# The eighth product saved in the down-projection instead of the up-projection, tokens on partitions there, and a last norm along columns

## Chip, cores and metric

One core of a Trainium2 chip runs the whole program: 512 tokens through two layers, each a mixer (attention, then a recurrent block) and an MLP, and a last norm. The metric is the device time of one execution in microseconds. The engines are called TensorE (PE, matmuls; PEld its weight loads), VectorE (DVE), ScalarE (ACT), GpSimd (POOL) and SyncE (SP, which issues most DMAs).

## The reference

`SEQ` is 512, `D_MODEL` 1024, `D_FF` 4096. The mixers are not changed and are left out here.

```python
def rmsnorm(x, g):
    xf = x.astype(jnp.float32)
    y = xf * lax.rsqrt(jnp.mean(xf * xf, axis=-1, keepdims=True) + RMS_EPS)
    return (y * g.astype(jnp.float32)).astype(x.dtype)
...
def sq_relu_mlp(h, w1, w2):
    z = jax.nn.relu(jnp.einsum('bsd,df->bsf', h, w1))
    return jnp.einsum('bsf,fd->bsd', z * z, w2)
...
    for layer in range(DEPTH):
...
        h = h + mix
        h = h + sq_relu_mlp(rmsnorm(h, norm_mlp[layer]), mlp_w1[layer], mlp_w2[layer])
    return rmsnorm(h, norm_final)
```

## The kernel before

Everything is float32, and every matmul is made of three: a float is split into a high part, which TensorE takes at full rate, and a low part, the rest, and `mm3` (L203) adds high x high, low x high and high x low. So each weight block is cast by ScalarE to its high part (`wh`, L134), and VectorE subtracts to get the low part (`wl`, L137). A block is 512 KB, 128 partitions x 1024 numbers. `plan` is the list of blocks in the order of use; `fetch` (L100) issues the DMA of one on SyncE's queue, then its cast and subtraction, and `want` keeps `ahead` blocks (6 in an MLP, else 4) fetched ahead of the matmuls. Blocks called `wr` are used as they come; blocks called `b` are raw ones from which sums are formed first (L130, L131).

The residual stream lies in `h` as eight tiles of 128 columns (features) on partitions by 512 tokens. `hnH` and `hnL` are its parts scaled by the norm's gain; the norm's row 1/sqrt(mean square) is multiplied in later, since it belongs to the token. A norm that is `flat` sums squares over partitions by two matmuls with a matrix of ones and then takes a root and a reciprocal (L264) on tiles of 128 x 512, so that each partition holds the row. The other form gets one number per token on partitions (L269) and turns it into a row by four small matmuls (L282).

An MLP (`mlp`, L604) handles the 4096 hidden features in eight groups of 512. The first group's up-projection is plain. Each of the other seven treats its 1024 x 512 weights and the 1024 x 512 tokens as two by two blocks and forms **seven products of half-size blocks in place of eight**, by sums and differences of blocks. The products (tiles `p`) are 128 x 256, each from sums of token halves (`tH`, `tL`, made once per layer from `h` by `sums_of`) and sums of weight blocks (`b`). VectorE puts the seven products together (tiles `cA`, `cB`, L677 to L694), multiplies by the row (L654), ScalarE squares (L645), and `z` holds the split result. The down-projection (`down`, L698) is plain: for each group and each of 8 column tiles `d`, 12 matmuls of 512 tokens, whose result VectorE adds to `h` (L704). `up(g)` is a generator: between its products the column tiles of group g-1 are placed, two after the second product, one after the next four, two after the last.

At the end of layer 0, `down` of the last group feeds the next norm tile by tile (`n1.feed`). The recurrent block then makes eight tiles `xb`, a convolution of them on VectorE (`xp`, L819, `xc`, L825), two gates by small matmuls (`ga`, `gx`), a scan, eight tiles `yb`, the product `gd` (L869), and the output blocks `ro`, whose results are added to `h` (L921). In the last layer the last group's down-projection is done in token halves, so that the first half's last norm (`nf0`) runs beside the second half (`nf1`); outputs are stored with features on partitions and the host transposes them.

The order of instructions on each engine is set by a scheduler after the program is written, with TensorE's order near the written one. PSUM tiles come from two rings of four banks, `mmp` and `atp`. TensorE waits where a bank it would write has not been read.

Of the kernel before, what the change touches and what calls it, by code (L numbers as in the profile page):

```python
# [31 lines left out]
C_MIX0, C_MLP0, C_MIX1, C_MLP1, C_FIN = 0, 8, 16, 24, 32  # L32
C_BIN, C_CW, C_CB, C_BGA, C_BGX, C_AP, C_BO = 40, 56, 88, 96, 104, 112, 120
# [7 lines left out]
def trunk(ctx: ExitStack, tc: tile.TileContext, xT, cols, win, wqkv, wo, rwin, rga, rgx, rwo, w1, w2, out):  # L41
# [17 lines left out]
    cst = per.tile([P, P], F32, name="cst")  # L59
    hT = []  # L60


    def residual(name):
        both = [per.tile([P, 4, T], F32, name=f"{name}{i}", tag=f"hx{i}") for i in range(2)]
        hT[:] = [both[k // 4][:, k % 4] for k in range(KT)]

# [5 lines left out]
    onesR = per.tile([P, P], F32R, name="onesR")  # L72
    epsb = per.tile([P, 1], F32, name="epsb")
    spare = per.tile([P, 1], F32, name="spare")
    rt = per.tile([P, 4], F32, name="rt")
    sp4 = per.tile([P, KT], F32, name="sp4")
# [8 lines left out]
    V.tensor_copy(onesR, ones)  # L85
# [11 lines left out]
    state = {"next": 0, "ready": [], "ahead": 4, "stop": None, "more": None, "units": 0}  # L97
    raws, start_ = {}, []

    def fetch():  # L100
# [4 lines left out]
        if state["more"] is not None:  # L105
            pool = state["more"] if state["units"] % 8 >= 5 else wsp
            state["units"] += 1
# [3 lines left out]
        if kind == "plain":  # L111
            n = nk * sum(src.shape[1] for src in srcs)
            raw = wraw.tile([P, 1024], F32, name=f"wr{i}", tag="wr")
            rv = raw[:, :n].rearrange("p (k c) -> p k c", k=nk)
            c0 = 0
            for n_, src in enumerate(srcs):
                w = src.shape[1]
                queue = nc.scalar if i == 0 and n_ else nc.sync
                queue.dma_start(rv[:, :, c0 : c0 + w], src.rearrange("(k p) c -> p k c", p=P))
                c0 += w  # L120
        else:
            if kind == "11":
                for name, src in zip(("11", "21", "22", "12"), srcs):
                    raws[name] = state["raw"].tile([P, 1024], F32, name=f"b{name}_{i}", tag=f"b{name}")
                    nc.sync.dma_start(raws[name].rearrange("p (k c) -> p k c", k=4), src.rearrange("(k p) c -> p k c", p=P))

            for name, at_, with_ in (("s1", "21", "22"), ("s2", "22", "11"), ("s4", "12", "22")):
                if kind == name:
                    if kind == "s1":
                        V.tensor_add(raws["11"], raws["11"], raws["21"])  # L130
                    V.tensor_add(raws[at_], raws[at_], raws[with_])  # L131
            raw = raws[{"s1": "21", "s2": "22", "s3": "11", "s4": "12"}.get(kind, kind)]
# [40 lines left out]
    def add_mlp(layer):  # L173
        starts.append(len(plan))
        for g in range(9):
            if g == 0:
                add(w1[layer], 0, 0, KT)
                add(w1[layer], 0, U, KT)
                continue
            if g < 8:  # L180
                rows, cs = (slice(0, T), slice(T, D)), (slice(g * T, g * T + U), slice(g * T + U, (g + 1) * T))
                srcs = [w1[layer][rows[k], cs[c]] for k, c in ((0, 0), (0, 1), (1, 1), (1, 0))]
                up_ = [(kind, 4, srcs) for kind in ("11", "s1", "12", "22", "s2", "s4", "s3")]
            else:
                up_ = []
            dn = [("plain", 4, [w2[layer][(g - 1) * T : g * T, u * U : (u + 1) * U]]) for u in range(4)]
            if up_:
                plan.extend(up_[0:2] + dn[0:1] + up_[2:3] + dn[1:2] + up_[3:5] + dn[2:3] + up_[5:7] + dn[3:4])
            else:
                plan.extend(dn)  # L190

    add_mlp(0)
    for u in range(8):
        add(rwin, 0, u * U, KT)
# [8 lines left out]
    def mm3(acc, WH, WL, XH, XL, start, stop):  # L203
        PE.matmul(acc, WH, XH, start=start, stop=False)  # L204
        PE.matmul(acc, WH, XL, start=False, stop=False)  # L205
        PE.matmul(acc, WL, XH, start=False, stop=stop)  # L206

    def project(accs, cols_, WH, WL, xs, mid=None):

        for k, (XH, XL) in enumerate(xs):  # L210
            if mid and k == 1:
                mid()
            for acc, c in zip(accs, cols_):
                mm3(acc, WH(k, c), WL(k, c), XH, XL, k == 0, k == len(xs) - 1)
# [5 lines left out]
    class Norm:  # L220
        def __init__(self, name, gain, c0=0, n=T, late=False, flat=False):
            self.name, self.gain, self.acc, self.last, self.c, self.n = name, gain, None, None, slice(c0, c0 + n), n
            self.late, self.flat = late, flat
# [6 lines left out]
        def square(self, k, apart=False):  # L230
            if self.acc is None:
                self.acc = wk.tile([P, T], F32, name=f"{self.name}acc", tag="nacc")[:, : self.n]
                S.activation(self.acc, hT[k][:, self.c], AF.Square)
            else:
                sq = wk.tile([P, T], F32, name=f"{self.name}sq{k}", tag="nsq", bufs=2)[:, : self.n]
                if apart:
                    self.mark = V.tensor_mul(sq, hT[k][:, self.c], hT[k][:, self.c])
                    self.last = sq
                    return
                S.activation(sq, hT[k][:, self.c], AF.Square)  # L240
                V.tensor_add(self.acc, self.acc, sq)

        def feed(self, k):
            if k == 0:
# [5 lines left out]


        def sums(self, room=lambda name: wk.tile([P, T], F32R, name=name, tag="nsq", bufs=2)):
            nt = self.n // P
            ss = atp(f"{self.name}ss")
            if self.flat:
                ss = ss[:, : self.n]
                aH, aL = (room(f"{self.name}a{i}")[:, : self.n] for i in range(2))
                S.copy(aH, self.acc)
                V.tensor_sub(aL, self.acc, f(aH))
                PE.matmul(ss, onesR, aH, start=True, stop=False)  # L260
                PE.matmul(ss, onesR, aL, start=False, stop=True)
                self.r = wk.tile([P, T], F32, name=f"{self.name}r", tag="nr")[:, : self.n]
                S.activation(self.r, ss, AF.Sqrt, bias=epsb, scale=1.0 / D)
                V.reciprocal(self.r, self.r)  # L264
                return
            parts = [self.acc] if self.last is None else [self.acc, self.last]
            for n, part in enumerate(parts):
                for t in range(nt):
                    PE.matmul(  # L269
                        ss[:, 2 * t : 2 * t + 2], part[:, t * P : (t + 1) * P], ones[:, 0:2],  # L270
                        start=n == 0 and t == 0, stop=n == len(parts) - 1, skip_group_check=True,
                    )
            S.activation(rt[:, :nt], ss[:, 0 : 2 * nt : 2], AF.Sqrt, bias=epsb, scale=1.0 / D)
            self.mark = V.reciprocal(rt[:, :nt], rt[:, :nt])

        def rstd(self):
            if self.flat:
                return self.r
            nt = self.n // P
            row = atp(f"{self.name}row")  # L280
            for t in range(nt):
                PE.matmul(row[:, t * P : (t + 1) * P], rt[:, t : t + 1].to_broadcast([P, P]), ident, start=True, stop=True)  # L282
            if self.last is not None:
                return row[:, : self.n]
            r = wk.tile([P, T], F32, name=f"{self.name}r", tag="nr")[:, : self.n]
            S.copy(r, row[:, : self.n])
# [4 lines left out]
    nm1 = Norm("nm1", C_MLP0, late=True, flat=True)  # L291
    with ExitStack() as actx:
# [72 lines left out]
        def wo_tile(m, acc, last):  # L365
            V.tensor_add(hT[m], acc, hT[m])
            if last:
                nm1.feed(m)
# [235 lines left out]
    def mlp(ly, norm, nxt, halves):  # L604
        with ExitStack() as mctx:
            pool = lambda name, bufs: mctx.enter_context(tc.tile_pool(name=f"{name}{ly}", bufs=bufs))
            sr, wx, tp, cp, zp = pool("sr", 1), pool("wx", 3), pool("t", 1), pool("c", 1), pool("z", 2)
            state.update(raw=sr, more=wx, units=0, ahead=6, stop=starts[ly + 1] + 4 if ly + 1 < len(starts) else None)
            z, r, tH, tL = {}, [], [], []

            def sums_of(k):
                g, g2 = (cst[:, norm.gain + j : norm.gain + j + 1] for j in (k, k + 4))
                a = wk.tile([P, T], F32, name=f"ha{ly}{k}", tag="nsq", bufs=2)
                S.activation(a, hT[k], AF.Copy, scale=g)
                H = tp.tile([P, 4, U], F32R, name=f"tH{ly}{k}", tag=f"tH{k}")
                L = tp.tile([P, 4, U], F32R, name=f"tL{ly}{k}", tag=f"tL{k}")
                raw = zp.tile([P, 2, T], F32, name=f"ht{ly}{k}", tag=("zH0", "zH1", "zL0", "zL1")[k])
                raw = raw.rearrange("p i (j c) -> p (i j) c", j=2)

# [357 lines left out]
```

## Time and profile before

| | us |
|---|---|
| median of 3 runs | 1079.86 (1078.96 to 1079.87) |
| the profiled execution | 1079.9 |
| its span | 1078.1 |
| MLP of layer 0, first up matmul to first matmul of the recurrent block | 245.8 to 584.3 |
| recurrent block | 584.3 to 727.8 |
| MLP of layer 1, to its last matmul's start | 727.8 to 1068.0 |

The mean clock granted to TensorE is 0.997. A row of groups reads: line, engine, operation, output and inputs by the program's names, shape, count, then busy time, mean nanoseconds of one, and the engine's idle time ahead of them with what ended it. A row of the timeline has the start and the duration first, both in microseconds. Matmul durations overlap, so the step from one start to the next is what a matmul costs when TensorE does not wait.

### The profile page before, as it was taken

To read this page: it belongs to the slowest core of one execution; us is meant where nothing else is said; L and a number is where in the kernel's file an instruction comes from. 1 tells how busy PE (TensorE), PEld (TensorE's weight loads), DVE (VectorE), ACT (ScalarE), POOL (GpSimd) and SP (SyncE) were. 2 spreads that over 40 slices of the span, in tenths; PEclk is the share of its full clock that TensorE was granted. 3 is DMA by queue.
4 is the path that set the end of the run, shared out by engine and by line. 5 is a ranking of instruction groups with operands and counts; after the bars stand their busy time and mean duration, and the time that the engine had idled before them with its cause. 6 is when DMAs were issued, how large, how long until landed. Compare 5 with 4: busy or idle time off the path is not lost.

```text
span 1078.1 us, 15331 instructions
## 1 busy us (share of the span) xinstructions
PE 1067.4 (99%) x6040; PEld 934.7 (87%) x6040; DVE 866.5 (80%) x1291; ACT 532.9 (49%) x778; POOL 9.7 (1%) x28
## 2 busy tenths in 40 slices
PE   9999999999999999999999999999999999999997
PEld 8788888888999999898988888888989999999896
DVE  6799779869987787776777989879887777786766
ACT  6667567556443343342444688356443343343322
POOL 1010000000000000000000000000000000000000
PEclk9999999999999999999999999999999999999998
DMA  8444253241432323323242222442431432322202
GB/s 268 106 135 131 67 176 98 79 156 59 138 117 79 117 87 108 101 80 97 69 127 78 80 61 77 147 146 65 143 121 64 137 96 81 113 88 87 66 1 79
DMA packets 112935, 111.15 MB, mean 103 GB/s; under 512 B 4192, under 2 KB 106720, under 8 KB 112864
## 3 DMA queue, kind: packets, MB, share of 16 engines
q1 hardware_dynamic: 112432, 109.85, 33.2%
q8 instruction: 47, 0.77, 0.3%
q10 hardware_dynamic: 432, 0.33, 0.1%
q14 instruction: 24, 0.20, 0.1%
HBM read 103.87 MB, written 2.10 MB: 98 GB/s over the span
## 4 chain that ended last, share of the span: by engine, by line
PE 92%; DVE 4%; DMA 2%; ACT 1%; issue 1%; SPq 0%; DVEq 0%; ACTq 0%
PE d L205 11%; PE d L204 11%; PE d L206 11%; PE p L206 9%; PE p L205 9%; PE p L204 9%; PE x L443 1%; PE wo L204 1%; PE wo L205 1%; PE ro L204 1%; PE ro L206 1%; PE wo L206 1%; PE xb L204 1%; PE xb L206 1%; PE xb L205 1%; PE u L204 1%
## 5 line engine op out<-in xcount | busy, mean ns | idle before, releaser
L134 ACT CAST wh<-wr 128x1024 fp32r<-128x1024 f32 (+1 forms) x129 | 133.5, 1038 | 203.5 <-PE d L205 89.2
L205 PE MATMUL d<-zL,wh 128*128 128x512 f32 (+1 forms) x544 | 205.8, 379 | 0.0
L204 PE MATMUL d<-zH,wh 128*128 128x512 f32 (+1 forms) x544 | 205.0, 379 | 0.0
L206 PE MATMUL d<-zH,wl 128*128 128x512 f32 (+1 forms) x544 | 204.7, 377 | 0.0
L134 ACT CAST wh<-b 128x1024 fp32r<-128x1024 f32 x98 | 101.4, 1047 | 166.2 <-PE p L205 81.1
L137 DVE TENSOR_TENSOR wl<-wr,wh 128x1024 fp32r<-128x1024 f32 (+1 forms) x130 | 156.2, 1204 | 25.0 <-ACT wh L134 24.6
L137 DVE TENSOR_TENSOR wl<-b,wh 128x1024 fp32r<-128x1024 f32 x98 | 118.6, 1220 | 39.4 <-ACT wh L134 39.2
L206 PE MATMUL p<-tH,wl 128*128 128x256 f32 x448 | 126.8, 283 | 0.0
L205 PE MATMUL p<-tL,wh 128*128 128x256 f32 x448 | 126.8, 283 | 0.0
L204 PE MATMUL p<-tH,wh 128*128 128x256 f32 x448 | 126.6, 283 | 0.0
L206 PEld LDWEIGHTS d<-zH,wl 128*128 128x128 f32 x544 | 102.3, 188 | 19.1
L204 PEld LDWEIGHTS d<-zH,wh 128*128 128x128 f32 x544 | 102.4, 189 | 16.7
L205 PEld LDWEIGHTS d<-zL,wh 128*128 128x128 f32 x544 | 102.6, 189 | 16.0 <-DVE zL L649 0.2
L704 DVE TENSOR_TENSOR h<-d,h 128x512 f32<-128x512 f32 x120 | 82.5, 687 | 39.0 <-PE d L206 38.2
L206 PE MATMUL p<-hnH,wl 128*128 128x256 f32 x336 | 95.1, 283 | 0.0
L205 PE MATMUL p<-hnL,wh 128*128 128x256 f32 x336 | 95.1, 283 | 0.0
L204 PE MATMUL p<-hnH,wh 128*128 128x256 f32 x336 | 94.9, 282 | 0.0
L205 PEld LDWEIGHTS p<-tL,wh 128*128 128x128 f32 x448 | 85.8, 192 | 1.7
L204 PEld LDWEIGHTS p<-tH,wh 128*128 128x128 f32 x448 | 85.8, 192 | 1.6
L206 PEld LDWEIGHTS p<-tH,wl 128*128 128x128 f32 x448 | 85.8, 192 | 0.0
L205 PEld LDWEIGHTS p<-hnL,wh 128*128 128x128 f32 x336 | 64.3, 191 | 1.7
L204 PEld LDWEIGHTS p<-hnH,wh 128*128 128x128 f32 x336 | 64.3, 191 | 1.6
(351 smaller groups left out, 2075.2 us busy)
## 6 DMA issues: line engine op xcount, KB each, us to landing
wr<-in_w SPq DMA_DIRECT2D x72, 512.0 KB, 3.5
b<-in_w SPq DMA_DIRECT2D x56, 512.0 KB, 4.1
wr<-in_wqkv SPq DMA_DIRECT2D x20, 512.0 KB, 4.1
wr<-in_rwin SPq DMA_DIRECT2D x16, 512.0 KB, 3.6
wr<-in_wo SPq DMA_DIRECT2D x8, 512.0 KB, 4.4
wr<-in_rwo SPq DMA_DIRECT2D x8, 512.0 KB, 3.4
x<-in_xT SPq DMA_DIRECT2D x8, 256.0 KB, 4.6
bias<-in_win SPq DMA_DIRECT2D x4, 512.0 KB, 4.6
```

The lines of the kernel that those rows point to most:

```text
L134: S.copy(H[:, :n], raw[:, :n])
L137: low = V.tensor_sub(L[:, :n], raw[:, :n], f(H[:, :n]))
L204: PE.matmul(acc, WH, XH, start=start, stop=False)
L205: PE.matmul(acc, WH, XL, start=False, stop=False)
L206: PE.matmul(acc, WL, XH, start=False, stop=stop)
L443: PE.transpose(b[:, c : c + P], pt[:, seg[t] + kt * P : seg[t] + (kt + 1) * P], ident)
L704: V.tensor_add(hT[m], acc, hT[m])
```

## The change

The up-projection becomes plain: 32 tiles `u` of 128 hidden features, each one block of 1024 x 128 weights and 24 matmuls of 512 tokens. ScalarE takes Relu and Square (L639, L640), without the norm's factor.

The down-projection takes the seven products. It runs in four rounds of 1024 hidden features. A round's weights are two by two blocks of 512 hidden features x 512 output columns; named 11, 21, 12, 22, they are kept as eight raw tiles of 512 KB in buffers of their own, and the differences t1 to t4 are formed in place on VectorE (L138). The activations' halves give s1 to s4 in the same way (L667, L679, L680, L682), and each operand is split into high and low (L660 on ScalarE, L661 on VectorE). Each product is 512 hidden features x 256 tokens x 512 columns, done as two tiles of 128 tokens. **The activations are now the stationary operand and the weights the moving one**, so a result has tokens on partitions and 512 columns along the row. Since the norm's factor is squared by the activation, the result is multiplied per token, hence per partition, by `rq`, the inverse of the mean square, while it is read and added to `dt` (L627; in layer 0 the first read of each tile is L625 on ScalarE). `dt` holds 512 tokens x 1024 columns in eight tiles.

The Strassen-like sums of products are formed in PSUM: bank pairs Y and X keep accumulating over several products, and are read after each. Y takes s1, then s4; X takes 11, s2, s3, 22; Z takes 12. Rounds 0 to 2 place one up tile of the next round after s1, s4, s2 and s3. Round 3 has none to place, and there each product is done for one token tile, read, and then for the other.

At the end of layer 0 (`turns`) 32 transposes bring `dt` back into `h` (`back`, L753, added at L755), and the first four `xb` tiles begin with the features 4 to 7 (`open_x`). The norm n1 is no longer flat: its row comes after the fourth xb tile, and the convolutions of the first four tiles follow it. At the start of layer 1 the residual is transposed into `dt` (`turn`, L618, ScalarE copy L619). At the end (`ends`) the last norm runs along the columns on tiles with tokens on partitions: a square with a sum along the row, a root, a reciprocal, one multiplication, and the store. The gain comes as a 128 x 1024 tensor from memory, and the output has tokens first.

The second ring of weight buffers has two blocks for three, and 5 are fetched ahead for 6.

```diff
-            if kind == "11":
-                for name, src in zip(("11", "21", "22", "12"), srcs):
-                    raws[name] = state["raw"].tile([P, 1024], F32, name=f"b{name}_{i}", tag=f"b{name}")
...
+            half, nk = nk, 2
+            if kind == "11" and half == 0:
+                for name, src in zip(("11", "21", "12", "22"), srcs):
+                    for h in range(2):
+                        raws[name, h] = state["raw"].tile([P, 1024], F32, name=f"b{name}{h}_{i}", tag=f"b{name}{h}")
...
+            at_, x, y = {
+                "t1": ("12", "12", "11"), "t2": ("22", "22", "12"), "t3": ("11", "22", "11"), "t4": ("21", "21", "22"),
+            }.get(kind, (kind, None, None))
+            raw = raws[at_, half]
+            if x:
+                V.tensor_sub(raw, raws[x, half], raws[y, half])
...
+        for p in range(4):
+            for j in range(4, 8):
+                up_(p, j)
...
+            for n, kind in enumerate(("11", "21", "t1", "22", "t2", "t3", "t4")):
+                for half in range(2):
+                    plan.append((kind, half, srcs))
+                if p < 3 and 2 <= n <= 5:
+                    up_(p + 1, n - 2)
...
+            def read(acc, t, c):
+                d, r = dt[t, c], rq[:, t : t + 1]
+                if (t, c) in new:
+                    new.remove((t, c))
+                    S.activation(d, acc, AF.Copy, scale=r)
+                else:
+                    V.scalar_tensor_tensor(d, acc, r, d, ALU.mult, ALU.add)
...
-                if (ly, g, n) == (0, 3, 1):
+                ins = V.tensor_sub(raw["s3"], raw["11"], raw["s1"])
...
+                    if j % 2:
+                        ks = slice(j - 5, j - 3)
+                        r = {n: raw[n][:, ks] for n in raw}
+                        V.tensor_sub(r["s2"], r["22"], r["s3"])
+                        V.tensor_sub(r["s4"], r["12"], r["s2"])
+                        split("12", ks)
+                        V.tensor_add(r["s1"], r["s1"], r["22"])
...
+                def step(name, bank, fresh, t0, c):
+                    if p < 3:
+                        product(name, bank, fresh)
+                    for t in range(2):
+                        if p == 3:
+                            product(name, bank, fresh, ts=(t,))
+                        read(bank[t], t0 + t, c)
...
+                step("11", X, True, 0, 0)
...
+                step("12", Z, True, 0, 0)
...
+                step("s1", Y, True, 2, 1)
...
+                ahead(0)
+                step("s4", Y, False, 0, 1)
...
+                ahead(1)
+                step("s2", X, False, 0, 1)
+                ahead(2)
+                if p == 3:
+
+                    (ends if ly else turns)(step, product, X)
+                    return
+                step("s3", X, False, 2, 1)
+                ahead(3)
+                step("22", X, False, 2, 0)
...
+                step("s3", X, False, 2, 1)
+                back(range(4), 0)
+                product("22", X, False, ts=(0,))
+                read(X[0], 2, 0)
+                back((2, 3), 1)
...
+                for i, t in enumerate((2, 3)):
+                    product("22", X, False, ts=(i,))
+                    read(X[i], t, 0)
+                    squares(t, 0)
+                    S.activation(total(t), total(t), AF.Sqrt, bias=part(t, 1), scale=1.0 / D)
+                    V.reciprocal(total(t), total(t))
+                    V.scalar_tensor_tensor(dt[t, 0], dt[t, 0], total(t), gain[0], ALU.mult, ALU.mult)
+                    store(t, 0, nc.sync)
...
-                if c == 1:
-                    cv[0] = conv(0, first)
-                if c >= 2:
+                if c == 2:
+                    n1.sums()
+                if c == 3:
+                    rr.append(n1.rstd())
+                    for j in range(4):
+                        cv[j] = conv(j, xbs[j])
```

**VectorE at the end of layer 0.** Before, the end of the down-projection is an addition, a split and a sum of squares for each column tile; these are the last rows, from the addition of the eighth tile to the first convolution product (`gL` is a gate weight, `nbin` a small pad).

```order
L704 TENSOR_TENSOR h_1566<-d_5619,h_1566 128x512
L137 TENSOR_TENSOR wl_5660<-wr_5661,wh_5659 128x1024
L228 SCALAR_TENSOR_TENSOR hnL_91<-h_1566,cst,hnH_83 128x512
L241 TENSOR_TENSOR n1acc<-n1acc,n1sq_5635 128x512
L814 TENSOR_TENSOR gL_5654<-graw_5652,gH_5653 128x512
L814 TENSOR_TENSOR gL_5698<-graw_5696,gH_5697 128x512
L259 TENSOR_TENSOR n1a_5709<-n1acc,n1a_5708 128x512
L820 COPY xp_5738<-nbin 128x3
L264 RECIPROCAL n1r<-n1r 128x512
L137 TENSOR_TENSOR wl_5666<-wr_5667,wh_5665 128x1024
L819 TENSOR_TENSOR xp_5738<-xb_5671,n1r 128x512
```

After, in the last round of layer 0, the queue from the low part of operand s2 to the first read of product s2 (bank `x_4675`) is this; `b` are weight differences, `wl` low parts, `d` the tiles `dt`, `y` the bank pair Y.

```order
L661 TENSOR_TENSOR gs_4794<-fs_4528,h2s_4793 128x1024
L138 TENSOR_TENSOR b_108_4485<-b_108_4497,b_108_4485 128x1024
L661 TENSOR_TENSOR fs_4798<-cs_4527,h0s_4797 128x1024
L138 TENSOR_TENSOR b_108_4487<-b_108_4487,b_108_4495 128x1024
L143 TENSOR_TENSOR wl_4802<-b_108_4485,wh_4801 128x1024
L627 SCALAR_TENSOR_TENSOR d_2579<-y_4673,rq,d_2579 128x512
L143 TENSOR_TENSOR wl_4807<-b_108_4487,wh_4806 128x1024
L627 SCALAR_TENSOR_TENSOR d_2581<-y_4674,rq,d_2581 128x512
L661 TENSOR_TENSOR c_4838<-a_4537,h_4837 128x1024
L138 TENSOR_TENSOR b_108_4489<-b_108_4489,b_108_4497 128x1024
L143 TENSOR_TENSOR wl_4847<-wr_4848,wh_4846 128x1024
L627 SCALAR_TENSOR_TENSOR d_2579<-x_4675,rq,d_2579 128x512
```

Where one addition per column tile stood, the read of a bank now has weight differences, weight lows and operand lows of 1024 ahead of it, the last of them the low of the recurrent block's first weights (`wr_4848`).

**TensorE at the same place.** The end of product s2's second token tile, the transposes back, and the start of product s3, which continues in `x_4675`:

```order
L216 MATMUL x_4676<-wl_4758,h2s_4793 128x512
L217 MATMUL x_4676<-wh_4757,gs_4794 128x512
L753 MATMUL back_4878<-ident,d_2578 128x128
L753 MATMUL back_4878<-ident,d_2580 128x128
L753 MATMUL back_4878<-ident,d_2578 128x128
L753 MATMUL back_4878<-ident,d_2580 128x128
L753 MATMUL back_4879<-ident,d_2578 128x128
L753 MATMUL back_4879<-ident,d_2580 128x128
L753 MATMUL back_4879<-ident,d_2578 128x128
L753 MATMUL back_4879<-ident,d_2580 128x128
L215 MATMUL x_4675<-wh_4762,h0s_4797 128x512
L216 MATMUL x_4675<-wl_4763,h0s_4797 128x512
```

Between the last matmul of one product and the first of the next in the same bank pair stand eight transposes of 128 x 128 and no up tile.

**TensorE at the norm of the recurrent block.** Before, the sums of squares stood three matmuls into the second tile `xb`:

```order
L206 MATMUL xb_5671<-hnH_83,wl_5441 128x512
L204 MATMUL xb_5703<-hnH_76,wh_5401 128x512
L205 MATMUL xb_5703<-hnL_84,wh_5401 128x512
L206 MATMUL xb_5703<-hnH_76,wl_5402 128x512
L260 MATMUL n1ss<-n1a_5708,onesR 128x512
L261 MATMUL n1ss<-n1a_5709,onesR 128x512
L204 MATMUL xb_5703<-hnH_77,wh_5401 128x512
```

After, the row stands behind the fourth tile (`xb_5052`) and ahead of the fifth (`xb_5350`):

```order
L215 MATMUL xb_5052<-hnH_79,wh_4938 128x512
L216 MATMUL xb_5052<-hnL_87,wh_4938 128x512
L217 MATMUL xb_5052<-hnH_79,wl_4939 128x512
L278 MATMUL n1row<-ident,rt 128x128 x4
L215 MATMUL xb_5350<-hnH_76,wh_4944 128x512
L216 MATMUL xb_5350<-hnL_84,wh_4944 128x512
```

VectorE's first convolution product, which needs the row, has moved with it from behind the second tile to behind the fourth.

More of the change, by code (lines that the diff above doesn't have):

```diff
@@ L104, in fetch @@
         pool = wsp
[L105 to L106 removed]
+        if state["more"] is not None and i < state["end"]:
+            pool = state["more"] if state["units"] % 7 >= 5 else wsp
             state["units"] += 1
@@ L248, in feed, with tokens @@
                 self.square(k)
-        def sums(self, room=lambda name: wk.tile([P, T], F32R, name=name, tag="nsq", bufs=2)):
-            nt = self.n // P
+        def tokens(self):
             ss = atp(f"{self.name}ss")
[L255 to L274, printed above, removed]
@@ L785, in trunk @@
-    n1 = Norm("n1", C_MIX1, flat=True)
-    mlp(0, nm1, n1.feed, False)
-    nm2 = Norm("nm2", C_MLP1, late=True, flat=True)
+            sr, zp, dp = (mctx.enter_context(tc.tile_pool(name=f"{n}{ly}", bufs=1)) for n in ("sr", "z", "d"))
+            wx = mctx.enter_context(tc.tile_pool(name=f"wx{ly}", bufs=2))
+            end = starts[ly + 1] if ly + 1 < len(starts) else None
+            state.update(raw=sr, more=wx, end=starts[ly] + 4 * 22, units=0, ahead=5, stop=end + 4 if end else None)
+            xs = [(hnH[k], hnL[k]) for k in range(KT)]
```

449 lines of the change are left out of this document (215 added, 234 removed).

## The prediction

> **What bounds the kernel now.** I read the page first (span, busy shares, chain), then the windows of the two MLP layers, the timeline of TensorE inside one of them, the waits, and last the tail.
>
> ```profile
> span 1078.1 us, 15331 instructions
> PE 1067.4 (99%) x6040; PEld 934.7 (87%) x6040; DVE 866.5 (80%) x1291; ACT 532.9 (49%) x778; POOL 9.7 (1%) x28
> PE 92%; DVE 4%; DMA 2%; ACT 1%; issue 1%; SPq 0%; DVEq 0%; ACTq 0%
> ```
>
> TensorE (PE) is the bound: busy for 99% of the span and 92% of the chain that ended last. VectorE (DVE) is second with 80%, which matters below. The execution took 1079.9 us, 1.8 more than its span and level with the median of 1079.86, so sums go from 1079.9.
>
> ```profile
> core 0: us, PE busy (x) PEld busy (x) DVE busy (x) ACT busy (x) POOL busy (x), PEclk, DMA share, GB/s
> 245.80:584.30 338.50, 338.50 (x2043) 303.37 (x2042) 271.11 (x335) 144.51 (x160) 0.00 (x0) 1.00 0.30 94
> 728.00:1068.30 340.30, 340.27 (x2140) 308.42 (x2138) 263.42 (x310) 135.53 (x153) 0.00 (x0) 1.00 0.27 86
> 596.20:690.80 94.60, 94.47 (x414) 77.24 (x414) 86.46 (x131) 67.30 (x92) 0.00 (x0) 1.00 0.25 78
> ```
>
> The columns are window, its length, then busy time of each engine. The first row is the MLP of layer 0 (first up matmul to last down matmul), the second that of layer 1, which starts at 727.8. In both TensorE never waits and VectorE is busy for 77 to 80%. A faster MLP therefore needs a shorter TensorE stream, and the 67 to 77 us in which VectorE rests are what a rearrangement may use up. What one matmul costs is its distance to the next:
>
> ```profile
> 470.06 0.28 PE L204 MATMUL p<-tH,wh 128*128 128x256 f32 x1
> ...
> 472.82 0.28 PE L206 MATMUL p<-tH,wl 128*128 128x256 f32 x1
> 472.94 0.40 PE L204 MATMUL d<-zH,wh 128*128 128x512 f32 x1
> ...
> 475.91 0.39 PE L205 MATMUL d<-zL,wh 128*128 128x512 f32 x1
> ```
>
> Each row is start, duration, engine, line. From the first p to the first d are 24 matmuls of 256 columns in 2.88 us: 0.120 each. From the first d to the last shown are 13 of 512 columns in 2.97 us: 0.228 each. So two half-wide matmuls cost 0.240 where a wide one costs 0.228, 5% more. The durations of 0.28 and 0.40 overlap and are not the price.
>
> **The matmuls that go and come.** Before, layer 0 has 864 wide and 1176 half-wide matmuls: 864 x 0.228 + 1176 x 0.120 = 338.1, the window's 338.5. Layer 1 has 768 and 1368 (its last group is in token halves): 339.3, and 340.5 measured from 727.8. Both forms save the same eighth, one in the up-projection, the other in the down-projection. Afterwards every product is 512 columns: 768 up and 4 rounds x 7 products x 24 = 672 down, 1440 x 0.228 = 328.3. New are 32 transposes per layer (back to columns in layer 0, to rows in layer 1) and four small norm matmuls.
>
> ```profile
> 82.53 1.09 PE x L443 x10
> 1068.44 0.58 PE L269 MATMUL nf1ss<-ones,nf1acc 128*128 128x2 f32 x4
> 1070.43 0.71 PE L282 MATMUL nf1row<-ident,rt 128*128 128x128 f32 x4 [0.55 <-DVE rt L274]
> ```
>
> Ten such transposes took 1.09, so 32 cost 3.5; the four small ones cost 0.5. That is 332.3 per layer. **Never waiting, TensorE saves 6.2 us in layer 0 and 8.2 in layer 1, 14.4 together.** In the recurrent layer a flat norm of two 512-column matmuls becomes one small and one row group (0.6 + 0.7 against 0.46): +0.8, half of which I expect to lie in the wait below, so +0.35.
>
> The row shows 0.120 and 0.228, with a clock of 1.00 in the window. The Trainium skill, page "TensorE: Matmul & The Clock Gate", section "Back-to-back issue gap", gives an isolated gap of N/2.4 + 2.5 ns, 109 and 216 ns here; by it the half-wide form would cost only 1% more and each layer would gain 0.1 to 0.3 us. The trace disagrees with it.
>
> **VectorE: what the new down-projection asks.** Its pace is read where it is saturated:
>
> ```profile
> 644.23 1.22 DVE L137 TENSOR_TENSOR wl<-wr,wh 128x1024 fp32r<-128x1024 f32 x1
> 645.37 0.74 DVE L825 SCALAR_TENSOR_TENSOR xc<-xp,cst,xc 128x512 f32<-128x512 f32 x1
> 646.03 0.68 DVE L841 TENSOR_TENSOR ix<-ix,xc 128x512 f32<-128x512 f32 x1
> 646.63 0.74 DVE L825 SCALAR_TENSOR_TENSOR xc<-xp,cst,xc 128x512 f32<-128x512 f32 x1
> ```
>
> Queued back to back, a 1024-wide subtraction takes 1.14 from start to start, a 512-wide three-operand one 0.66, a plain one 0.60. Now the reads of the product banks, the weight differences and the operand halves all fall into the down part of a round, where products of different names share a bank. In rounds 0 to 2 four up units of 5.47 us lie between the products, so in each such round's down part (11 x 5.47 = 60 us) VectorE owes 18 weight lows, 8 differences and 5 operand lows of 1024 (35.3) and 14 reads (9.2), some 45: covered. **In the last round no up unit is left.** Products 11, 12, s1, s4, s2 take 5 x 24 x 0.228 = 27.4 us from the end of the last up unit; then s3's first half needs the bank that s2's first half filled, so its read must be done. Up to and with that read VectorE's queue holds 31 instructions in layer 0: 4 operand steps of 512 (2.4), 9 reads (5.9), and 18 of width 1024 (6 weight differences, 5 operand lows, 7 weight lows: 20.5), 28.8 in all. It can begin some 2.4 us after the up unit (a queued ScalarE cast, Relu, Square):
>
> ```profile
> L134 ACT CAST wh<-b 128x1024 fp32r<-128x1024 f32 x98 | 101.4, 1047 | 166.2 <-PE p L205 81.1 <-DVE b L131 52.8 <-DMA b<-in_w 18.9
> L828 ACT CAST xcH<-xc 128x512 fp32r<-128x512 f32 x8 | 4.9, 618 | 5.5 <-DVE xc L825 5.5
> ```
>
> So 1.05 + 2 x 0.62. The read ends near 31.3; TensorE is there at 27.4 + 8 back-transposes (0.9) = 28.3. **Stall: 3.0 us in layer 0.** In layer 1 neither the first low of the next layer's weights (1.14) nor the transposes are there: 30.1 against 27.4, **2.7 us**. What else is queued behind the read (later weight lows, the read of the second half) is late by the same amount and stays 0.8 us ahead of product 22. The bounds are 0, if VectorE starts its differences before the up unit ends, and 5.5, if each of the 31 pays its full duration (0.08 more, 2.5).
>
> The Trainium skill, page "Perfetto Trace Analysis", section "Matmuls", wants independent groups to rotate through PSUM banks so that the evacuation overlaps. The last round does it only across token halves, 2.74 us of cover; by this rule a wait at each reuse is what to expect, and the stall terms above are of that kind.
>
> **Into the recurrent layer.** Before, the first convolution product starts 11.9 us after the first xb matmul (584.31); now all four first xb blocks come before the norm's row, so it starts some 22 us after.
>
> ```profile
> 584.31 0.39 PE L204 MATMUL xb<-hnH,wh 128*128 128x512 f32 x1
> 596.25 1.28 DVE L819 TENSOR_TENSOR xp<-xb,n1r 128x512 f32<-128x512 f32 x2
> 683.84 0.40 PE L204 MATMUL ro<-gdH,wh 128*128 128x512 f32 x1
> 689.49 1.28 DVE L869 TENSOR_TENSOR gdL<-y,gdH 128x512 fp32r<-128x512 f32 x2
> ```
>
> Two costs follow. First, the sixth xb block needs the bank of xb0, freed only by VectorE's first xp product, which stands behind a weight low, the row and its copy. From the end of xb3 on these are 0.7 (row), a ScalarE cast of 1.05 and copy some 0.7 (estimated from the 512-wide cast above), a low of 1.14, two products of 0.6, and hand-overs, about 7.9, while TensorE has xb4 (5.47) to do: **2.45 us**. Second, VectorE owes 86.5 us between its first xp product and the gated halves gd5 (the window's busy time); TensorE has xb4 to xb7 21.9, gates 10.9, yb 43.8 and half of the first output block 11.0 = 87.6 until it needs them. That cover was 94.6 us. The lag is between 0 and 7 us, and since VectorE can't be saturated throughout, I take **1.5**. Together +4.3 with the row, bounds 0.4 to 10.
>
> **Layer starts** cost nothing: the 512-wide reciprocals (3.35 us, three of them) go, and the transposes of layer 1 stand behind up units. **DMA**: the same bytes.
>
> ```profile
> wr<-in_w SPq DMA_DIRECT2D x72, 512.0 KB, 3.5
> b<-in_w SPq DMA_DIRECT2D x56, 512.0 KB, 4.1
> ```
>
> A block lands 3.5 to 4.1 us after its issue. SP asks for a new round's block 11 when the low of t3 is made; the next round's first difference stands 7 rows later on VectorE, and what is queued behind it (a low, four reads) is due only after about 10 us. Covered, unless blocks come 10 us late.
>
> **The tail.**
>
> ```profile
> 1068.01 0.28 PE L206 MATMUL d<-zH,wl 128*128 128x256 f32 x1
> 1068.33 0.42 DVE L773 TENSOR_TENSOR h<-d,h 128x256 f32<-128x256 f32 x1
> 1069.27 0.61 PE L269 MATMUL nf1ss<-ones,nf1sq 128*128 128x2 f32 x4 [0.26 <-DVE nf1sq L237]
> 1069.92 0.26 ACT L273 ACTIVATE rt<-nf1ss,epsb 128x2 f32<-128x2 f32 x1 [2.09 <-PE nf1ss L269]
> 1070.21 0.17 DVE L274 RECIPROCAL rt<-rt 128x2 f32<-128x2 f32 x1 [0.20 <-ACT rt L273]
> 1071.18 3.22 DVE L758 SCALAR_TENSOR_TENSOR nf1o<-h,cst,nf1row 128x256 f32<-128x256 f32 x8
> ```
>
> Before: 9.8 us from the last matmul's end (1068.3) to 1078.1, of which two passes through TensorE and 3.2 us of scaling go. After: read 0.75, Square with its sum 0.7 (no row shows that form; between the 512-wide cast's 0.62 and twice that, taken near the first, since one pass does both), root 0.26, reciprocal 0.17, scaling 0.75, hand-overs 0.7, and the store, which before took 3.7 us past the last scaling (1074.4): 7.0 to 7.8, taken as 7.4, **-2.4 us**.
>
> **Sum.** -14.4 + 3.0 + 2.7 + 4.3 - 2.4 = -6.8, so 1073.1; I say **1073**.
>
> **Rivals.**
> (a) *VectorE is never late*: the differences, which need no up unit, run early, and the recurrent stage has room. The 23% of rest in the windows speaks for it, the 31-row queue against it. 1079.9 - 14.4 + 0.35 - 2.4 = 1063.5.
> (b) *VectorE does not keep its queued pace, slower than before.* Every low waits for ScalarE's cast of the same block:
>
> ```profile
> L137 DVE TENSOR_TENSOR wl<-b,wh 128x1024 fp32r<-128x1024 f32 x98 | 118.6, 1220 | 39.4 <-ACT wh L134 39.2
> ```
>
> 0.4 us of idle per low plus the unoverlapped 0.08. In the last rounds that adds 2.5 from pace and 7 lows x 0.4 = 2.8 each; in the recurrent stage the lag becomes 7, not 1.5 (+5.5). Together 1073 + 10.6 + 5.5 = 1089; it decides from 9 us on, about half of that price, so 1082 to 1089.
> (c) *Round changes wait for weight blocks*: only past 10 us after issue; eight blocks are 4.2 MB, and 2 us late at six changes would give 1085. The median of 4.1 speaks against.
> (d) *The half-wide form is not dearer* (the issue gap of the page named above): the 14.4 vanish, 1087. The p and d rows speak against it.
>
> **How the numbers follow.** Forecast (1069 to 1077.7) 0.52; (a) 0.17; a mild form of (b), within 0.2% of before (2.2 us, about what a measurement of this kernel tells from no change), 0.12; (b) proper 0.12; (c) 0.05; (d) 0.02. Faster 0.69, same 0.12, slower 0.19. The range 1063 to 1084 reaches to (a) and into (b).
>
> **What would show it.** In the trace after: 1440 matmuls of 512 columns at 0.228 per MLP; one stall near 3 us on x ahead of s3 in each last round, its releaser a VectorE read (L627); one of 2 to 3 us at the sixth xb block, released by an xp product; the output blocks ro waiting for gd by up to 7 us; 7.4 us after the last matmul. Wrong would make it: waits in rounds 0 to 2, a down pitch above 0.228, or a recurrent stage longer by over 10 us.

## The result and the profile after

The changed kernel takes 1073.21 us (median of 6 runs, 1071.31 to 1074.74) against 1079.86 (6 runs, 1078.96 to 1080.17): a ratio of 0.9938, 95% interval 0.9926 to 0.9951. The forecast was 1073. The profiled execution took 1074.2 us, 1 us above the median, with a span of 1072.4.

The first lines of its page, and its chain by engine, answer to those of before:

```profile
span 1072.4 us, 12842 instructions
PE 1056.1 (98%) x4820; PEld 875.6 (82%) x4820; DVE 799.9 (75%) x1168; ACT 587.2 (55%) x886; POOL 9.0 (1%) x28
PE 92%; DVE 6%; ACT 1%; issue 1%; DMA 0%; POOL 0%; ACTq 0%; POOLq 0%
```

TensorE (PE) is busy for 11.3 us less, and the share of VectorE (DVE) in the chain has grown from 4 to 6%: there are waits now. Its windows, with the MLP of layer 0, the recurrent block, the MLP of layer 1, and three short stretches that are explained below (length, then busy time of each engine, then the clock granted to TensorE):

```profile
core 0: us, PE busy (x) PEld busy (x) DVE busy (x) ACT busy (x) POOL busy (x), PEclk, DMA share, GB/s
244.70:579.80 335.10, 332.02 (x1473) 274.78 (x1472) 237.40 (x276) 168.27 (x205) 0.00 (x0) 0.99 0.30 90
579.80:729.20 149.40, 147.41 (x649) 120.73 (x648) 129.89 (x188) 96.83 (x136) 0.00 (x0) 0.99 0.36 115
729.20:1065.10 335.90, 333.07 (x1480) 275.23 (x1480) 228.61 (x248) 163.84 (x210) 0.00 (x0) 0.99 0.27 83
565.80:569.20 3.40, 3.40 (x10) 2.66 (x9) 3.40 (x4) 0.00 (x0) 0.00 (x0) 0.52 0.45 150
606.90:610.10 3.20, 3.20 (x10) 2.42 (x9) 2.99 (x7) 1.04 (x2) 0.00 (x0) 0.50 0.49 163
1054.10:1057.50 3.40, 3.40 (x10) 2.63 (x9) 0.80 (x3) 2.45 (x9) 0.00 (x0) 0.51 0.00 0
```

The MLPs are 3.4 and 4.3 us shorter, the recurrent block is 5.9 longer (143.5 before; about one of them is transposes that now lie behind its first matmul). The waits of TensorE by what released them, with their sum, number and the longest:

```profile
PE x L215 <- DVE d L627: 5.9, 2, 3.1
...
PE xb L215 <- DVE xp L866: 1.9, 1, 1.9
```

The first are the two that the prediction places ahead of product s3. In the timeline of TensorE around the one in layer 0 (start, duration), it waits 3.08 us for the read of s2's bank, restarts, and two matmuls later falls to half its pace:

```profile
561.30 1.03 PE L753 MATMUL back<-ident,d 128*128 128x128 f32 x8
565.41 0.47 PE L215 MATMUL x<-wh,h0s 128*128 128x512 f32 x1 [3.08 <-DVE d L627]
565.72 0.45 PE L216 MATMUL x<-wl,h0s 128*128 128x512 f32 x1
565.97 0.63 PE L217 MATMUL x<-wh,fs 128*128 128x512 f32 x1
566.40 0.63 PE L215 MATMUL x<-wh,h0s 128*128 128x512 f32 x1
...
568.96 0.57 PE L215 MATMUL x<-wh,h0s 128*128 128x512 f32 x1
569.37 0.40 PE L216 MATMUL x<-wl,h0s 128*128 128x512 f32 x1
```

From 565.97 to 569.37 eight matmuls take 3.40 us, 0.425 each and not 0.227, so 1.6 us are lost: that is the window with a clock of 0.52. The same comes 1.6 us after the wait in layer 1 and 0.7 us after the one in the recurrent block, each again with 1.6 us lost. These are the ends of those two waits:

```profile
606.44 0.50 PE L215 MATMUL xb<-hnH,wh 128*128 128x512 f32 x1 [1.88 <-DVE xp L866]
...
1052.75 0.47 PE L215 MATMUL x<-wh,h0s 128*128 128x512 f32 x1 [2.83 <-DVE d L627]
```

Ahead of s3 in layer 0 VectorE works without a pause; these are its last rows ahead of the read:

```profile
561.12 1.22 DVE L661 TENSOR_TENSOR c<-a,h 128x1024 fp32r<-128x1024 f32 x1
562.25 1.22 DVE L138 TENSOR_TENSOR b<-b,b 128x1024 f32<-128x1024 f32 x1
563.39 1.22 DVE L143 TENSOR_TENSOR wl<-wr,wh 128x1024 fp32r<-128x1024 f32 x1
564.52 0.75 DVE L627 SCALAR_TENSOR_TENSOR d<-x,rq,d 128x512 f32<-128x512 f32 x1
```

An operand low, a weight difference, the low of the recurrent block's first weights, then the read that ends at 565.27 and releases TensorE. The tail after the last matmul's start is 7.26 us (1065.14 to 1072.4), against 10.1 before.

### The profile page after: what moved, and what is told of

Its sections match the earlier page's. It is cut to its first block, busy times and chain, and to the rows that moved or that the text cites. A ratio compares the mean times of both kernels' runs of the same rounds, so it can differ in the third digit from the quotient of the medians.

```text
span 1072.4 us, 12842 instructions
## 1 busy us (share of the span) xinstructions
PE 1056.1 (98%) x4820; PEld 875.6 (82%) x4820; DVE 799.9 (75%) x1168; ACT 587.2 (55%) x886; POOL 9.0 (1%) x28
## 4 chain that ended last, share of the span: by engine, by line
PE 92%; DVE 6%; ACT 1%; issue 1%; DMA 0%; POOL 0%; ACTq 0%; POOLq 0%
PE u L215 11%; PE u L216 11%; PE u L217 11%; PE x L215 5%; PE x L217 5%; PE x L216 5%; PE y L215 2%; PE y L216 2%; PE y L217 2%; PE x L437 2%; PE xb L215 1%; PE xb L217 1%; PE xb L216 1%; PE wo L215 1%; PE wo L216 1%; PE ro L215 1%
## 5 line engine op out<-in xcount | busy, mean ns | idle before, releaser
L215 PE MATMUL u<-hnH,wh 128*128 128x512 f32 x512 | 200.3, 391 | 0.0
L217 PE MATMUL u<-hnH,wl 128*128 128x512 f32 x512 | 199.6, 390 | 0.0
L216 PE MATMUL u<-hnL,wh 128*128 128x512 f32 x512 | 199.4, 390 | 0.0
L217 PEld LDWEIGHTS u<-hnH,wl 128*128 128x128 f32 x512 | 96.1, 188 | 20.3
L215 PEld LDWEIGHTS u<-hnH,wh 128*128 128x128 f32 x512 | 96.1, 188 | 19.7
L216 PEld LDWEIGHTS u<-hnL,wh 128*128 128x128 f32 x512 | 96.2, 188 | 19.6
L138 DVE TENSOR_TENSOR b<-b,b 128x1024 f32<-128x1024 f32 x64 | 76.7, 1223 | 1.3 <-DMA b<-in_w 1.3
L215 PE MATMUL x<-wh,h 128*128 128x512 f32 x128 | 50.1, 391 | 0.0
L216 PE MATMUL x<-wl,h 128*128 128x512 f32 x128 | 50.0, 390 | 0.0
L627 DVE SCALAR_TENSOR_TENSOR d<-x,rq,d 128x512 f32<-128x512 f32 x60 | 42.8, 745 | 3.5 <-PE x L217 3.5
L639 ACT ACTIVATE a<-u 128x512 f32<-128x512 f32 x64 | 37.8, 590 | 13.3 <-PE u L217 13.3
L640 ACT ACTIVATE a<-a 128x512 f32<-128x512 f32 x64 | 40.6, 635 | 1.8
L660 ACT CAST h<-a 128x1024 fp32r<-128x1024 f32 (+1 forms) x32 | 26.8, 836 | 6.5 <-PE y L216 5.7
```

The source lines that it names most:

```text
L138: V.tensor_sub(raw, raws[x, half], raws[y, half])
L215: PE.matmul(acc, WH, XH, start=start, stop=False, skip_group_check=more)
L216: PE.matmul(acc, WH, XL, start=False, stop=False, skip_group_check=more)
L217: PE.matmul(acc, WL, XH, start=False, stop=stop, skip_group_check=more)
L627: V.scalar_tensor_tensor(d, acc, r, d, ALU.mult, ALU.add)
L639: S.activation(c, acc.rearrange("p (h c) -> p h c", h=2), AF.Relu)
```

## Experiments

The theory, Q: ahead of s3 TensorE waits for VectorE's queue, one for one, and the queue is full because of weight differences made late. A second, C, was added when the half clock was seen: the wait itself causes it. Rivals stand in each expectation. All ratios are to the kernel before, run on the same chip: 1079.38 us for the first four, 1079.31 for the last three.

**e1_more.** In the last round of each MLP two lows are computed twice.

```diff
-                    V.tensor_sub(L[:, ks], raw[n][:, ks], f(H[:, ks]))
+                    for _ in range(2 if p == 3 and n in ("s3", "22") else 1):
+                        V.tensor_sub(L[:, ks], raw[n][:, ks], f(H[:, ks]))
```

> In the last round of each MLP the operand lows of s3 and 22 are computed twice (same result), two more 1024-wide VectorE instructions ahead of the read of s2 on which TensorE waits. Theory Q (the stall is VectorE's queue, one for one): in layer 1 the wait ahead of s3 grows from 2.8 by 2 x 1.14 to about 5.1 us; in layer 0, where one weight low also moves ahead of the read, from 3.1 by 3 x 1.14 to about 6.5; the time rises by 5 to 6 us. Rival R (TensorE waits for something else that comes at its own time, a weight block or a cast, and the read only happens to be last): both waits stay within 1 us of what they were, and the time rises by less than 2.

Measured: 1080.87 us, ratio 1.0009 (1.0000 to 1.0019), 7.7 above the changed kernel. The two waits:

```profile
PE x L215 <- DVE d L627: 10.9, 2, 5.8
...
1059.17 0.76 PE L215 MATMUL x<-wh,h0s 128*128 128x512 f32 x1 [5.09 <-DVE d L627]
```

The wait in layer 1 is 5.09 against 5.1 expected, that in layer 0 5.8 against 6.5; there the read is late by the expected 3.4 us, but 0.6 of it TensorE spends in and ahead of the transposes. R falls. The median rose by 2.7 us more than the waits (10.9 for 5.9); the mean clock was 0.990 to 0.994 in its runs, against 0.993 to 0.997. Between the two profiled executions the rise is 6.1 us (1080.3 for 1074.2), most of it waits and transposes (5.6). Behind the wait of 5.8 us the half clock lasted 5.5 us:

```profile
568.70:574.20 5.50, 5.50 (x13) 4.34 (x14) 3.98 (x6) 0.00 (x0) 0.00 (x0) 0.51 0.63 193
```

**e2_fill.** TensorE gets useless work where it waits.

```diff
                 if p == 3:
+                    idle = mmp(f"idle{ly}")
+                    H, (WH, WL) = low["s2"][0], held["s2"][1]
+                    for n in range(12):
+                        PE.matmul(idle, H[:, 3, 0:P], WH(1, slice(0, T)), start=n == 0, stop=n == 11)
                     (ends if ly else turns)(step, product, X)
```

> In the last round of each MLP, 12 matmuls of 512 columns into a spare bank, whose result nothing uses, stand between product s2 and what follows it: TensorE works 2.7 us where it idled 2.8 to 3.1. Theory C (the half clock seen 0.6 to 1.3 us after each wait comes from the wait itself): the runs of 7 to 9 matmuls at 0.427 behind those two places vanish, the ones behind the norm's row in the recurrent block stay, and the time falls by about 3 us against the changed kernel (2 x 1.5) although not one wait is removed; runs below 1070 become possible. Rival P (the clock falls by chance or by load): the half-clock matmuls remain, or come elsewhere, and the time is that of the changed kernel or up to 0.5 longer.

Measured: 1070.70 us, ratio 0.9920 (0.9905 to 0.9935), four runs from 1069.65 to 1071.86. At the place shown above:

```profile
561.76 2.89 PE L736 MATMUL idle<-wh,h2s 128*128 128x512 f32 x12
564.48 1.03 PE L756 MATMUL back<-ident,d 128*128 128x128 f32 x8
565.88 0.47 PE L215 MATMUL x<-wh,h0s 128*128 128x512 f32 x1 [0.36 <-DVE d L627]
566.18 0.40 PE L216 MATMUL x<-wl,h0s 128*128 128x512 f32 x1
566.42 0.40 PE L217 MATMUL x<-wh,fs 128*128 128x512 f32 x1
```

Product s3 still begins 4.1 us after s2's end, but no matmul behind it is at half pace, here or in layer 1. The half-clock matmuls behind the row in the recurrent block stay. The four runs show mean clocks of 0.997 to 0.998, the changed kernel's 0.993 to 0.997. Work that computes nothing made the kernel 2.5 us faster (1.9 by the two ratios, since the kernel before ran 0.5 faster beside this run): C holds.

**e3_pool.** The differences of the last round on GpSimd.

```diff
...
-                V.tensor_sub(raw, raws[x, half], raws[y, half])
+                (G if i in late else V).tensor_sub(raw, raws[x, half], raws[y, half])
```

> The eight weight differences of the last round of each MLP run on GpSimd, not VectorE: 6 of them stood ahead of the read of s2, 6.8 us of VectorE's queue. Theory Q: both waits ahead of s3 go (to under 0.3 us) and with them the half clock behind them; 2 x (2.8 to 3.1) + 2 x 1.5 less, so about 9 us below the changed kernel, 1064. Rival G (GpSimd is slower at it or hinders VectorE, since no row shows such an instruction there): the weights come late and TensorE waits for a cast, in place of the read; time same or slower than the changed kernel.

Measured: 1086.62 us, ratio 1.0068 (1.0053 to 1.0083): the rival's side. The waits ahead of s3 are gone, but TensorE waits earlier, ahead of s1 and s4, up to 3.4 us at a time. GpSimd's group, then VectorE's timeline beside it:

```profile
L139 POOL TENSOR_TENSOR b<-b,b x16: 2342/3035/3727, 484.5 to 1047.2; 128x1024 f32<-128x1024 f32 x16
```

```profile
536.42 0.69 DVE L682 TENSOR_TENSOR fs<-a,cs 128x512 f32<-128x512 f32 x1
537.07 2.86 DVE L664 TENSOR_TENSOR nn<-a,h 128x512 fp32r<-128x512 f32 x1
539.85 2.88 DVE L683 TENSOR_TENSOR gs<-a,fs 128x512 f32<-128x512 f32 x1
542.65 2.88 DVE L685 TENSOR_TENSOR a<-a,a 128x512 f32<-128x512 f32 x1
545.45 0.74 DVE L630 SCALAR_TENSOR_TENSOR d<-x,rq,d 128x512 f32<-128x512 f32 x1
```

One difference takes 3.0 us (the median, between 2.3 and 3.7), and while GpSimd makes three of them, from 536.6 to 545.0, VectorE's 512-wide subtractions take 2.9 us each and not 0.68. The three cost VectorE 6.6 us more, about as much as the six differences that had been taken off its queue (6 x 1.14 = 6.8).

**e4_xb4.** The fifth `xb` block is written ahead of the gates.

```diff
...
                     rr.append(n1.rstd())
+                    early.update(w=want(2), acc=atp("xb4"))
+                    project([early["acc"]], PAIR[0:1], *early["w"], xs)
                     for j in range(4):
```

> The fifth xb block takes its bank ahead of the gates, so that TensorE can do it between the norm's row and the block that needs xb0's bank. Theory B (the wait of 1.9 us behind the row is for xb0's bank, freed by the first xp product 1.9 us after the row): 5.5 us of work cover it, the wait and the half clock behind it vanish, about 3.4 us below the changed kernel. Rival L (VectorE's debt in the recurrent block is the limit): the wait comes back further on, at a gate or at the output blocks, and the time falls by less than 1 us.

Measured: 1075.50 us, ratio 0.9968 (0.9955 to 0.9980), so 2.3 above the changed kernel (3.2 by the two ratios). The wait behind the row is gone, and is back 55 us later:

```profile
662.51 0.50 PE L215 MATMUL yb<-hnH,wh 128*128 128x512 f32 x1 [2.58 <-DVE y L910]
```

There a `yb` block needs a bank that VectorE has not read; no half clock follows this wait. Rival L holds in that the wait comes back: in the changed kernel VectorE is busy for 86 of the 90 us from 610 to 700, and a wait that is covered at one end of this stage comes out at the other. Why the median rose, where L had it fall by less than 1 us, stays open; the profiled execution, at 1074.0, is the fastest of six.

**e5_free.** In the last round t2 goes into another buffer. t2 was written over block 22, so it had to wait until 22's own low part was made; written over t1, it need not. In the changed kernel the last low part ahead of the first of the six differences, by the order of the blocks that of 22's first half, waits for ScalarE's cast, and VectorE has nothing else to do meanwhile:

```profile
535.05 1.23 DVE L143 TENSOR_TENSOR wl<-b,wh 128x1024 fp32r<-128x1024 f32 x1 [4.21 <-ACT wh L140]
```

```diff
+                "T2": ("12", "22", "12"), "T3": ("11", "12", "11"), "T4": ("21", "21", "12"),
...
-            for n, kind in enumerate(("11", "21", "t1", "22", "t2", "t3", "t4")):
+            kinds = ("11", "21", "t1", "22", "t2", "t3", "t4") if p < 3 else ("11", "21", "t1", "22", "T2", "T3", "T4")
+            for n, kind in enumerate(kinds):
```

> In the last round only, the difference t2 is written over t1 (no longer needed) in place of over block 22, and t3, t4 take it from there. The differences then wait for no low part of 22 and stand ahead of the last up unit's results on VectorE, where it has room: the 6 x 1.14 us leave the queue between the last up unit and the read of s2, with the same instructions in total and none on GpSimd. Theory Q: the read is done near 24.6 us after the last up unit, before TensorE asks for it at 27.4 to 28.3; both waits ahead of s3 go to under 0.3, the half clock behind them too, and the time falls by 2 x 3.0 + 2 x 1.5 = 9 to about 1064. Rival T (VectorE's total of the round is what counts): the waits come back at an earlier product or at 22, and the time falls by less than 3.

Measured: **1064.30 us, ratio 0.9856 (0.9841 to 0.9870)**, 8.9 us below the changed kernel, with the same number of instructions on VectorE (busy 799.9 us in both) and the same matmuls. The six differences now run ahead of the last up unit's results, four of them in one go. In the timeline of layer 0's last round, the read of s2's first half is over at 561.4, and s3 starts at 562.09, right behind s2:

```profile
532.22 4.75 DVE L139 TENSOR_TENSOR b<-b,b 128x1024 f32<-128x1024 f32 x4
...
560.65 0.74 DVE L629 SCALAR_TENSOR_TENSOR d<-x,rq,d 128x512 f32<-128x512 f32 x1
...
562.09 0.39 PE L217 MATMUL x<-wh,h0s 128*128 128x512 f32 x1
```

```profile
PE xb L217 <- DVE xp L868: 1.9, 1, 1.9
```

The second fence, from its waits, is the one in the recurrent block. Apart from 1.0 us at the program's start it is the only wait of TensorE above 0.5 us that is left. T falls: not the total of the round counts, but when it can be done. This kernel beats both.

**e6_swap.** As e5_free, with product s2 ahead of s4 in the last round.

```diff
+            kinds = ("11", "21", "t1", "22", "t2", "t3", "t4") if p < 3 else ("11", "21", "t1", "T2", "22", "T3", "T4")
...
+                if p == 3:
+                    step("s2", X, False, 0, 1)
                 step("s4", Y, False, 0, 1)
...
```

> As e5_free, and in the last round product s2 comes before s4, so that the same bank pair is never used by two products in a row up to s3. Theory Q: where e5_free has no wait left, nothing more is gained, within 0.5 us of it. Rival K (the cover of 2.74 us by the other token tile is itself too short, whatever the queue): e5_free keeps waits of 0.3 to 1 us ahead of s4 and s3 that this one has not, and this one is 1 to 2 us faster.

Measured: 1064.29 us, ratio 0.9860 (0.9844 to 0.9877). The same as e5_free: rival K falls, and with the queue short the other token tile is cover enough.

**e7_freerow.** As e5_free, with 8 idle matmuls behind the norm's row.

```diff
...
                     rr.append(n1.rstd())
+                    idle = atp("idle")
+                    for n in range(8):
+                        PE.matmul(idle, WH(0, PAIR[0]), xs[0][0], start=n == 0, stop=n == 7)
                     for j in range(4):
```

> As e5_free, and 8 matmuls of 512 columns into a spare bank, with a result that nothing uses, stand behind the norm's row in the recurrent block, where TensorE waits 1.9 us for the first xp product. Theory C (a wait of 1.9 us is enough for the half clock): the wait stays as long as it was (8 x 0.23 = 1.8 us are filled), but the 7 half-clock matmuls behind it vanish: 1.4 us below e5_free in its median, and less spread between runs. Rival: the time is that of e5_free, or up to 0.5 longer because the filled bank moves the gates.

Measured: 1064.17 us, ratio 0.9856 (0.9842 to 0.9871), from 1063.72 to 1064.75 where e5_free had 1062.64 to 1065.23. The half-clock matmuls behind the row are gone from its trace and the spread is smaller, but the median fell by 0.1, not 1.4. In e5_free two runs of four show a clock of 0.997 (both 1065.23) and two 0.998 and 0.999 (1062.64, 1063.36), so its median already holds half of the loss; and the added matmuls may cost something too (its fastest run is 1.1 above e5_free's), which was not taken apart. As to time this run decides nothing.

## Why the prediction was right, and where not

By the terms of its sum, profiled execution against profiled execution:

| term | predicted, us | measured, us |
|---|---|---|
| TensorE's work, with the norm's row | -14.05 | -14.4 (what the other rows leave of -5.7) |
| wait ahead of s3, layer 0 | +3.0 | +3.1 |
| wait ahead of s3, layer 1 | +2.7 | +2.8 |
| wait at the xb block | +2.45 | +1.9 |
| lag at the gated halves | +1.5 | 0 |
| tail | -2.4 | -2.8 |
| half clock behind the waits | none | +4.8 (three stretches of 1.6) |
| start of layer 0's MLP | 0 | -1.1 |
| sum | -6.8 | -5.7 |

*The work* of TensorE came out: half-wide products for wide ones is worth what 0.120 against 0.228 says, some 14 us. The rival by which the half-wide form is not dearer is out. That row is a remainder, and no kernel with this part alone was run.

*The waits ahead of s3* had the right place, size and cause. The read was forecast at 31.3 us after the last up unit and ended 31.3 us after it (product 11 starts at 533.99, the read ends at 565.27); its 31 rows took 29.1 us, from 536.21 on, for 28.8. e1 shows that they follow VectorE's queue one for one, and e5 that the queue's content, not the bank's reuse, is what was late. Rival (a), VectorE never late, was the wrong forecast for this order and the right one for the order of e5_free: its 1063.5 against 1064.3. That it is so near is in part luck, since e5_free still has the wait of 1.9 us in the recurrent block, which (a) has at nothing. The prediction took the place of the differences in the queue as given; that an in-place write put them there was not seen.

*The wait in the recurrent block* was right in the bank (xb0's, freed by the first xp product) and nearly in size, but not in its working. The prediction had TensorE do the fifth block meanwhile (5.47 us) and a chain of 7.9 us. In the trace the block behind the row already waits for xb0's bank, so it is the sixth (`xb_5350`, called the fifth above); the fifth, whose bank belongs to the gates first, comes later. The chain is short:

```profile
603.49 1.04 ACT L140 CAST wh<-wr 128x1024 fp32r<-128x1024 f32 x1 [2.40 <-PE xb L216]
603.51 1.05 PE L278 MATMUL n1row<-ident,rt 128*128 128x128 f32 x8
604.56 1.23 DVE L143 TENSOR_TENSOR wl<-wr,wh 128x1024 fp32r<-128x1024 f32 x1 [3.26 <-PE n1row L278]
605.71 1.28 DVE L866 TENSOR_TENSOR xp<-xb,n1acc 128x512 f32<-128x512 f32 x2
```

The cast runs beside the row, a low and the first product follow, and TensorE restarts at 606.44, 2.9 us after the end of xb3 and not 7.9. The named parts of the 7.9 add up to 4.8; the other 3.1, put down to hand-overs, had no row behind them. A cover of 5.5 us that was not there and a chain 5.0 us too long cancelled: that the size came out is luck.

*The lag at the gated halves* did not come, though VectorE was as full as foreseen; e4 shows that there is no room left.

*The half clock* was missing from the sum. By the mean clocks of the runs (last section) it would also be why the time varies by 3.4 us between runs of the changed kernel, of which only one has a trace. It hid that the other terms together were 3.7 us too dear (-10.5 without it, for -6.8). The median run, with two stretches by its clock, holds two thirds of it. That the forecast met it to 0.2 us is partly luck.

*The tail* was mis-sized by 0.4. *The start*: the MLP began 1.1 us earlier; in the experiments' traces, with the same code up to there, it began between 244.1 and 245.6, so this is scatter. The rivals on slow VectorE and on late weight blocks did not occur: all 64 differences together waited 1.3 us for a block.

```profile
L138 DVE TENSOR_TENSOR b<-b,b 128x1024 f32<-128x1024 f32 x64 | 76.7, 1223 | 1.3 <-DMA b<-in_w 1.3
```

## What to carry to other kernels

When the work of the busiest engine is shortened, make a timetable of the second engine's queue for each stretch without cover, up to the instruction that the first one waits for; here 31 rows gave the wait to 0.1 us. Then ask of each row why it can't stand earlier: a result that is written over an operand still in use waits for that operand's last reader, and another free buffer as its target was worth 8.9 us with not one instruction fewer. A wait of TensorE may cost more than its length.

## What the runs showed of the hardware

In the changed kernel each wait of TensorE of 1.9 to 3.1 us was followed, 0.6 to 1.6 us after it ended, by 3.2 to 3.4 us at a clock of 0.50 to 0.52, some 1.6 us lost each. Ahead of two of these three waits stands 1.0 us of 128 x 128 matmuls (the transposes, the norm's row); whether these count as work was not tried, and from the last 512-column matmul on the gaps are 4.1, 3.0 and 2.9 us. The drop does not follow every time: the wait of 2.58 us in e4_xb4's trace has none behind it, and the six runs of the changed kernel lie in three pairs by mean clock, 0.997 (1071.31, 1071.46), 0.995 (1073.17, 1073.25) and 0.993 (1074.18, 1074.74), which fits one, two and three such stretches: the profiled one, at 0.993, has three, and e5_free's, at 0.997, one. The mean clock is a rough sign: it takes in the end of the program behind the last matmuls, where the kernel before, at 0.997, has its only stretch at 0.50. The Trainium skill, page "TensorE: Matmul & The Clock Gate", section "HAM oscillation — how this bites in real kernels", asks for no idle gap above some 3.4 us; by that rule these waits, all shorter, would be free, and here they were not. Its "What's actually happening" speaks of a free-running window of about 3.4 us, which agrees with the length of the stretches in the changed kernel and with their coming and going between runs, but not with the 5.5 us at 0.51 behind the longer wait of e1_more; which phase decides was not tried.

While GpSimd made 1024-wide subtractions at 3.0 us each, VectorE's 512-wide ones took 2.9 us against 0.68 (e3_pool).
